# A trunk kernel on one core: six turns per mixer moved from TensorE to transposing DMAs on ScalarE's queue

## The chip, the core and the metric

The kernel runs on one core of a Trainium2 chip. Times are microseconds (us) of device time of that core. Five engines run their own instruction streams, in order: TensorE (PE; its weight loads are listed as PEld), VectorE (DVE), ScalarE (ACT), GpSimd (POOL) and SyncE (SP, which here only issues DMAs). They wait for each other by semaphores. Lower is better.

## The reference

Two layers over x of 256 tokens by 1024 features, in float32. Each layer is a half-step feed-forward network (FFN), a mixer, and a second half-step FFN, each with a norm before and after it. The mixer projects the normed x to 3080 columns and splits them:

```
da_q, da_k, da_v, ml_qk, ml_v, ml_o, ml_g = jnp.split(proj, SPLIT_IDX, axis=-1)
y_da = _diff_attention(da_q, da_k, da_v, lam_vecs, subln_g, lam_init)
y_ml = _mlstm(ml_qk, ml_v, ml_o, ml_g, conv_w, conv_b, gate_b, ml_norm_g)
y = jnp.concatenate([y_da, y_ml], axis=-1).astype(h.dtype)
return y @ w_out
```

In the attention half, queries and keys are rotated (each 64-wide head by position), the queries are scaled by 1/8, and the scores of two softmaxes per head are combined. In the other half, ml_qk (512 columns) goes through a causal convolution of width 4 along the tokens, then silu, and gives queries and keys of a gated linear recurrence. Attention scores and the convolution need the features on partitions, while the projection gives tokens on partitions: so rotated queries, rotated keys and ml_qk have to be turned (transposed), each for both blocks t of 128 tokens. These are six turns of 128 x 512 in each mixer.

## The kernel before

Every float32 product is made of three matmuls: weights and activations are split into a rounded part (wh, hh) and the rest (wl, hl). Weights come in pieces of 1 MB (wr, three buffers) on SP's queue. For each half of a piece ACT makes wh (line 288) and DVE makes wl (line 289). Lines 401 to 403 are the three matmuls.

**FFN.** Its 11 chunks of 256 hidden columns are walked one after the other. After silu and product, the hidden values h are turned by a DMA: ACT writes the two 16-bit words of each float apart into planes (line 535), SP issues a transposing DMA from planes to a tile turned (line 537), and DVE joins the words again into hT (line 539). The last chunk is computed in turned form and needs no turn, so one FFN has ten.

**Mixer.** The function traverse walks the projection in steps of one k (three matmuls) and puts the other work between them: the tuple AT gives, for each stage in the list of stages, the step ahead of which it is written down. A scheduler then orders each engine's stream. The stages of interest:

- conv_input(t) copies ml_qk of token block t out of PSUM into nat (line 895). conv_input_t(t) turns nat by four PE transposes into a PSUM bank ptr (line 879, in the function transposed), and ACT copies the bank into xpad (line 899). Then conv runs on DVE (line 910).
- rope(pin, t) copies a query or key block to rv (ACT, line 1057), and DVE rotates it: lines 1058, 1063 twice, and the sum at line 1064 into ra. roped(i, t) turns ra by four PE transposes, and ACT copies the bank into qkT with a scale (line 1071).
- The gate stages: gate_copy (line 930, ACT), gate_inputs (PE line 939, DVE lines 940 and 942), gate_logs (ACT), gate_log_f (DVE line 957, into g2), gate_rows (PE line 967, four transposes of g2), gate_chain (DVE from line 973 on).
- weighted_qk (PE lines 1023 to 1031, DVE lines 1028, 1027, 1033), scores (PE line 1094; DVE lines 1097 and 1098), combine (DVE line 1122, PE line 1124).

Names: pieces 35 and 36 are the weights of the queries, 37 and 38 those of the keys. q0, q1, k0, k1 below are the rotated query and key blocks t = 0, 1. The tag "ev" has five buffers for nat, ra, rb, rv, h, planes, turned, hT and others. The tag "bk" has four PSUM banks.

Of the kernel before, what the change touches and what calls it, by code (L numbers as in the profile page):

```python
# [19 lines left out]
U16 = mybir.dt.uint16  # L20
AF = mybir.ActivationFunctionType
ALU = mybir.AluOpType
# [3 lines left out]
P = 128  # L26
D = 1024
S = 256
NT = S // P
# [10 lines left out]
AT = (0, 2, 6, 6, 7, 22, 24, 24, 24, 24, 36, 40, 24, 46, 34, 50, 43, 52, 52, 57, 61, 60, 61, 67, 67, 69, 71, 78, 74, 74, 78, 84)  # L40
# [91 lines left out]
class _Trunk:  # L132
# [397 lines left out]
    def ffn_planes(self, h):  # L530


        nc = self.nc
        planes = self.t2("planes", (P, 2, 512), U16)
        nc.scalar.activation(planes, h.rearrange("p t j -> p (t j)").bitcast(U16).rearrange("p (n u) -> p u n", u=2), AF.Copy)
        turned = self.t2("turned", (P, 8, P), U16)
        nc.sync.dma_start_transpose(turned, planes.rearrange("p u n -> p (u n)"))
        hT = self.t2("hT", (P, 4, P))
        nc.vector.tensor_copy(hT.rearrange("p b n -> p (b n)").bitcast(U16).rearrange("p (n u) -> p u n", u=2),  # L539
                              turned.rearrange("p (u b) n -> p u (b n)", u=2))  # L540
        ops = [self.ffn_operand() for _ in range(NT)]
        for t in range(NT):
            self.ffn_hilo(hT[:, 2 * t:2 * t + 2], *ops[t])
        return [[tuple(v[:, k] for v in ops[t]) for k in range(2)] for t in range(NT)]

# [157 lines left out]
    def mixer(self, pre, gi_post):  # L703
        m = _Mixer(self, pre, gi_post // 3)
# [10 lines left out]
        m.conv_input_t(0)  # L715
# [42 lines left out]
class _Mixer:  # L758


    def __init__(self, tr, pre, l):
        self.tr, self.l = tr, l
        self.xT, self.r = pre
        self.yT = [[None, None] for _ in range(NT)]
        self.conved = None
        self.rot, self.qkT, self.so, self.p = [], [], [], {}
# [62 lines left out]
    def stages(self):  # L829
# [6 lines left out]
            self.gate_rows,  # L836
            self.gate_chain,
# [6 lines left out]
            lambda: self.roped(0, 0, 0.125),  # L844
            self.conv_silu,
            lambda: self.roped(0, 1, 0.125),
            self.weighted_qk,
            lambda: self.roped(1, 0, 1.0),
            lambda: self.scores(0, 0),
            self.intra_weights,  # L850
            lambda: self.roped(1, 1, 1.0),
# [37 lines left out]
    def conv_input(self, t, pin):  # L889
        tr = self.tr  # L890
        if t == 0:
            self.xpad = tr.xpad
        nat = tr.t2("nat")
        with tr.tc.high_priority():
            self.act(nat, pin, AF.Copy, scale=self.r[t])
        self.nat = nat

    def conv_input_t(self, t):
        self.act(self.xpad[:, :, 3 + t * P:3 + (t + 1) * P], self.transposed(self.nat), AF.Copy)
# [152 lines left out]
    def rope(self, pin, t):  # L1052
        tr, tt = self.tr, self.tt
        v, a, b = tr.t2("rv"), tr.t2("ra"), tr.t2("rb")
        v8, a8, b8 = (i.rearrange("p (g d) -> p g d", g=8) for i in (v, a, b))
        with tr.tc.high_priority():
            self.rv = self.act(v, pin, AF.Copy, scale=self.r[t])
# [7 lines left out]
        self.rot.append(a)  # L1065

    def roped(self, i, t, scale):

        if t == 0:
            self.qkT.append(self.tr.t4("qkT", (P, 4, S)))  # L1070
        self.act(self.qkT[i][:, :, t * P:(t + 1) * P], self.transposed(self.rot[2 * i + t]), AF.Copy, scale=scale)
# [185 lines left out]
```

## Time and profile before

| what | value |
|---|---|
| median of 3 runs | 962.49 us (962.29 to 962.94) |
| the profiled execution, its own time | 962.02 us |
| its span, first to last instruction | 960.2 us |
| PE busy | 952.8 us (99%) |
| DVE busy, ACT busy | 638.7 us, 571.2 us |
| granted TensorE clock, mean | 0.999 |
| transposing DMAs | 40, all issued by SP |
| first mixer, second mixer | about 195 to 290 us, about 668 to 763 us |

A row of the timeline gives start, duration, engine, line, operation, and names out<-in; "x4" stands for four in a row, then the duration is from the first start to the last end. In brackets stands how long the engine had been idle and who ended that. A row of the table of groups gives busy time, mean ns of one, and idle time before. Matmuls overlap in the records: one of 512 columns lasts 0.39 us, but the next starts 0.23 us later. A neighbour on DVE or ACT may start about 0.08 us before the one ahead has ended.

### The profile page before, as it was taken

How to read it: one execution, taken by the hardware profiler on the slowest of the kernel's cores; microseconds unless marked ns; L12 is line 12 of the kernel's file. 1: busy time of each engine (PE TensorE's matmuls, PEld its weight loads, DVE VectorE, ACT ScalarE, POOL GpSimd, SP SyncE). 2: the span in 40 equal slices, each digit the busy share in tenths (PEclk: the TensorE clock that was granted, in tenths of full speed). 3: DMA queues.
4: the chain of work that ended last, by engine and by line, in shares of the span. 5: the costliest groups of instructions: out<-in, count | busy, mean ns of one | idle time of the engine just before them, and what ended most of it. 6: DMA issues, size and time to landing. Idle time of an engine off the chain costs nothing.

```text
span 960.2 us, 12037 instructions
## 1 busy us (share of the span) xinstructions
PE 952.8 (99%) x4523; PEld 788.9 (82%) x4523; DVE 638.7 (67%) x945; ACT 571.2 (59%) x937; POOL 29.5 (3%) x55
## 2 busy tenths in 40 slices
PE   9999999999999999999999999999999999999997
PEld 7888888888888888888888888888888888888885
DVE  6765655689867766555687555566988676755553
ACT  8755554577856655454476555555778466555542
POOL 2000000000010000000000000000001000000000
PEclk9999999999999999999999999999999999999999
DMA  8996656236352975676458666653454257765621
GB/s 317 328 288 202 225 193 219 105 132 241 116 192 91 299 245 193 218 247 176 154 189 283 206 225 208 196 187 128 172 202 174 90 182 256 272 205 192 225 72 44
DMA packets 69879, 189.32 MB, mean 197 GB/s; under 512 B 45274, under 2 KB 46426, under 8 KB 49086
## 3 DMA queue, kind: packets, MB, share of 16 engines
q1 hardware_dynamic: 69246, 187.95, 58.0%
q8 instruction: 35, 0.57, 0.2%
q10 hardware_dynamic: 576, 0.61, 0.2%
q14 instruction: 22, 0.18, 0.1%
HBM read 177.01 MB, written 1.05 MB: 185 GB/s over the span
## 4 chain that ended last, share of the span: by engine, by line
PE 97%; DVE 1%; DMA 1%; ACT 0%; issue 0%; POOLq 0%; DVEq 0%; ACTq 0%
PE pin L401 13%; PE pin L402 13%; PE pin L403 13%; PE bk L401 10%; PE bk L402 10%; PE bk L403 10%; PE ptr L402 6%; PE ptr L403 6%; PE ptr L401 6%; PE pin L610 1%; PE ptr L610 1%; PE ptr L879 1%; PE ptr L427 1%; DMA wr<-in_w_dram 1%; PE bk L1094 1%; PE ptr L615 1%
## 5 line engine op out<-in xcount | busy, mean ns | idle before, releaser
L289 DVE TENSOR_TENSOR wl<-wr,wh 128x1024 fp32r<-128x1024 f32 x324 | 389.2, 1221 | 180.4 <-ACT wh L288 174.4
L288 ACT ACTIVATE wh<-wr 128x1024 fp32r<-128x1024 f32 x324 | 333.9, 1055 | 171.2 <-DMA wr<-in_w_dram 44.1
L401 PE MATMUL pin<-wh,both 128*128 128x512 f32 x560 | 221.2, 396 | 0.0
L403 PE MATMUL pin<-wh,both 128*128 128x512 f32 x560 | 218.3, 390 | 0.0
L402 PE MATMUL pin<-wl,both 128*128 128x512 f32 x560 | 218.2, 390 | 0.0
L401 PE MATMUL bk<-wh,hh 128*128 128x512 f32 x352 | 137.4, 390 | 0.1
L402 PE MATMUL bk<-wl,hh 128*128 128x512 f32 x352 | 137.0, 389 | 0.0
L403 PE MATMUL bk<-wh,hl 128*128 128x512 f32 x352 | 136.9, 389 | 0.0
L403 PEld LDWEIGHTS pin<-wh,both 128*128 128x128 f32 x560 | 105.1, 188 | 22.3
L401 PEld LDWEIGHTS pin<-wh,both 128*128 128x128 f32 x560 | 105.3, 188 | 22.0 <-issue 0.7
L402 PEld LDWEIGHTS pin<-wl,both 128*128 128x128 f32 x560 | 105.3, 188 | 20.6
L403 PE MATMUL ptr<-wh,both 128*128 128x512 f32 x256 | 99.4, 389 | 0.0
L402 PE MATMUL ptr<-wl,both 128*128 128x512 f32 x256 | 99.4, 389 | 0.0
L401 PE MATMUL ptr<-wh,both 128*128 128x512 f32 x256 | 98.9, 389 | 0.0
L401 PEld LDWEIGHTS bk<-wh,hh 128*128 128x128 f32 x352 | 66.1, 188 | 14.0 <-ACT hh L550 0.5
L403 PEld LDWEIGHTS bk<-wh,hl 128*128 128x128 f32 x352 | 66.1, 188 | 13.7
L402 PEld LDWEIGHTS bk<-wl,hh 128*128 128x128 f32 x352 | 66.1, 188 | 13.5
L539 DVE COPY hT<-turned 128x1024 uint16<-128x1024 uint16 x40 | 30.3, 757 | 41.9 <-DMA turned<-planes 41.5
L401 PEld LDWEIGHTS ptr<-wh,both 128*128 128x128 f32 x256 | 48.1, 188 | 10.0
L402 PEld LDWEIGHTS ptr<-wl,both 128*128 128x128 f32 x256 | 48.1, 188 | 10.0
L550 ACT ACTIVATE hh<-hT 128x256 fp32r<-128x256 f32 x80 | 28.9, 409 | 46.0 <-DVE hT L539 46.0
L403 PEld LDWEIGHTS ptr<-wh,both 128*128 128x128 f32 x256 | 48.1, 188 | 9.9
(210 smaller groups left out, 891.9 us busy)
## 6 DMA issues: line engine op xcount, KB each, us to landing
wr<-in_w_dram SPq DMA_DIRECT2D x162, 1024.0 KB, 5.2
gpost<-in_gpost_dram SPq DMA_DIRECT2D x6, 512.0 KB, 6.3
wr<-in_w_dram SPq DMA_DIRECT2D x2, 512.0 KB, 6.1
wr<-in_w_dram SPq DMA_DIRECT2D x3, 256.0 KB, 4.3
x<-in_x_dram SPq DMA_DIRECT2D x3, 256.0 KB, 4.4
turned<-planes SPq DMA_TRANSPOSE x40, 4.4
out_dram<-x SPq DMA_DIRECT2D x2, 256.0 KB, 2.1
x<-in_x_dram SPq DMA_DIRECT2D x2, 128.0 KB, 3.0
```

Source lines behind the costliest of these rows:

```text
L288: ia = nc.scalar.activation(hi, raw[:, j], AF.Copy)
L289: iv = nc.vector.tensor_tensor(lo, raw[:, j], hi.bitcast(F32), op=ALU.subtract)
L401: mm(ps, xh, wh, start=start, stop=False)
L402: mm(ps, xh, wl, start=False, stop=False)
L403: mm(ps, xl, wh, start=False, stop=stop)
L427: nc.tensor.transpose(ptr[:, k, :], x[:, (4 * hf + k) * P:(4 * hf + k + 1) * P], self.ident)
L539: nc.vector.tensor_copy(hT.rearrange("p b n -> p (b n)").bitcast(U16).rearrange("p (n u) -> p u n", u=2), turned.rearrange("p (u b) n -> p ...
L550: self.nc.scalar.activation(hh, h, AF.Copy)
L610: self.nc.tensor.matmul(b, self.cols(w[kh], k)[0][:, c], both[kh][:, k].rearrange("p i t -> p (i t)"), start=kh == 0 and k == 0, stop=Fals ...
L615: self.nc.tensor.matmul(b[:, 0:NT * P], self.cols(w[kh], k)[1][:, c], both[kh][:, k, 0:NT].rearrange("p i t -> p (i t)"), start=False, sto ...
L879: self.T(ptr[:, b, :], a[:, b * P:(b + 1) * P], self.tr.ident)
L1094: self.mm(pcs[c][:, h, :], self.qkT[0][rows, h0 + h, t * P:(t + 1) * P], self.qkT[1][rows, h0 + h, 0:nk], start=True, stop=True)
```

## The change

The six turns of each mixer leave PE. A new function turn(v, queue, planes) does what ffn_planes did, but sends the transposing DMA back into the tile v itself, whose words are already in planes; joined(out, turned) is the copy on DVE that puts the words together, in the mixer straight into xpad or qkT. In the mixer the queue is ScalarE's, so ACT issues these DMAs; rb serves as planes for the rotated blocks. The scale 1/8 of the queries moves from the copy into qkT to the copy into rv, with a small extra DVE instruction for its factor (rhalf). FFN keeps SP's queue and now also turns in place, so the tile turned is gone. AT is renumbered for the stages whose place changes.

```diff
-AT = (0, 2, 6, 6, 7, 22, 24, 24, 24, 24, 36, 40, 24, 46, 34, 50, 43, 52, 52, 57, 61, 60, 61, 67, 67, 69, 71, 78, 74, 74, 78, 84)
+AT = (0, 2, 6, 6, 7, 20, 22, 24, 24, 24, 24, 36, 40, 28, 46, 34, 50, 46, 52, 52, 57, 61, 60, 61, 67, 67, 69, 71, 78, 74, 74, 78, 84)
...
+    def turn(self, v, queue, planes=None):
+        planes = (planes if planes is not None else self.t2("planes")).bitcast(U16).rearrange("p (u n) -> p u n", u=2)
+        u16 = v.bitcast(U16)
+        self.nc.scalar.activation(planes, u16.rearrange("p (n u) -> p u n", u=2), AF.Copy)
+        turned = u16.rearrange("p (b n) -> p b n", b=8)
+        queue.dma_start_transpose(turned, planes.rearrange("p u n -> p (u n)"))
+        return turned
+
+    def joined(self, out, turned):
+        self.nc.vector.tensor_copy(out.bitcast(U16).rearrange("p b (n u) -> p u b n", u=2),
+                                   turned.rearrange("p (u b) n -> p u b n", u=2))
...
-        m.conv_input_t(0)
...
             self.gate_rows,
+            lambda: self.conv_input_t(0),
             self.gate_chain,
...
             self.act(nat, pin, AF.Copy, scale=self.r[t])
-        self.nat = nat
+        self.nat.append(tr.turn(nat, tr.nc.scalar))
...
-        self.act(self.xpad[:, :, 3 + t * P:3 + (t + 1) * P], self.transposed(self.nat), AF.Copy)
+        self.tr.joined(self.xpad[:, :, 3 + t * P:3 + (t + 1) * P], self.nat[t])
...
+        scale = self.r[t]
+        if len(self.rot) < NT:
+            scale = tr.small("rhalf", (P, 1))
+            self.ts(scale, self.r[t], 0.125, None, op0=ALU.mult)
...
-        self.rot.append(a)
+        self.rot.append(tr.turn(a, tr.nc.scalar, b))
...
-        self.act(self.qkT[i][:, :, t * P:(t + 1) * P], self.transposed(self.rot[2 * i + t]), AF.Copy, scale=scale)
+        self.tr.joined(self.qkT[i][:, :, t * P:(t + 1) * P], self.rot[2 * i + t])
```

Three places in the streams show what the scheduler made of it (the second mixer has the same rows under other numbers). In brackets stand the semaphores that a row waits for: of an engine by its name, of a DMA as DMAHW.

First, DVE at the start of the first mixer, before: the second half of the pre-norm of token block 1, piece 36, the gate inputs, piece 37, g2, and the first row of the gate chain.

```order
L433 TENSOR_TENSOR both_179_1700<-xg_199_1829,both_179_1700 128x4x128 [waits Activation_49]
L289 TENSOR_TENSOR wl_36_0_1863<-wr_36_1861,wh_36_0_1864 128x1024 [waits DMAHW5_49,Activation_49]
L289 TENSOR_TENSOR wl_36_1_1867<-wr_36_1861,wh_36_1_1868 128x1024 [waits Activation_49]
L940 TENSOR_REDUCE gs_208_1896<-bk_207_1895 128x16 [waits PE_49]
...
L289 TENSOR_TENSOR wl_37_0_1982<-wr_37_1980,wh_37_0_1983 128x1024 [waits DMAHW6_49,Activation_49]
L957 SCALAR_TENSOR_TENSOR g2_591<-gn_209_1897,lg_210_1917 128x4x4 [waits Activation_49]
L957 SCALAR_TENSOR_TENSOR g2_591<-gn_209_1897,lg_210_1917 128x4x4
L289 TENSOR_TENSOR wl_37_1_1992<-wr_37_1980,wh_37_1_1993 128x1024 [waits Activation_49]
L973 SCALAR_TENSOR_TENSOR gt_221_2011<-c_scan_570,bk_211_1931 100x256 [waits PE_49]
```

The same place now:

```order
L433 TENSOR_TENSOR both_169_1690<-xg_190_1822,both_169_1690 128x4x128 [waits Activation_49]
L551 COPY xpad_608<-nat_185_1803 128x2x4x128 [waits DMAHW0_49]
L289 TENSOR_TENSOR wl_36_0_1850<-wr_36_1848,wh_36_0_1851 128x1024 [waits DMAHW5_49,Activation_49]
L289 TENSOR_TENSOR wl_36_1_1854<-wr_36_1848,wh_36_1_1855 128x1024 [waits Activation_49]
L948 TENSOR_REDUCE gs_198_1883<-bk_197_1882 128x16 [waits PE_49]
...
L289 TENSOR_TENSOR wl_37_0_1976<-wr_37_1974,wh_37_0_1977 128x1024 [waits DMAHW6_49,Activation_49]
L289 TENSOR_TENSOR wl_37_1_1986<-wr_37_1974,wh_37_1_1987 128x1024 [waits Activation_49]
L965 SCALAR_TENSOR_TENSOR g2_588<-gn_199_1884,lg_200_1904 128x4x4 [waits Activation_49]
L965 SCALAR_TENSOR_TENSOR g2_588<-gn_199_1884,lg_200_1904 128x4x4
L981 SCALAR_TENSOR_TENSOR gt_214_2010<-c_scan_567,bk_201_1918 100x256 [waits PE_49]
```

The join into xpad stands ahead of piece 36 and waits for its DMA, and both halves of piece 37 now stand ahead of g2.

Second, DVE ahead of the scores, before: the rotation of k0 (ra_234) and k1 (ra_238), and qd, whose reading sets a PSUM bank free.

```order
L289 TENSOR_TENSOR wl_41_1_2250<-wr_41_2223,wh_41_1_2251 128x1024 [waits Activation_49]
L1064 TENSOR_TENSOR ra_234_2100<-ra_234_2100,rb_235_2101 128x512 [waits DVE_49]
L1058 TENSOR_TENSOR ra_238_2136<-rv_237_2135,c_1_568 128x512 [waits Activation_49]
L1063 TENSOR_TENSOR rb_239_2137<-rv_237_2135,c_1_568 128x8x32 x2
L289 TENSOR_TENSOR wl_42_0_2324<-wr_42_2322,wh_42_0_2325 128x1024 [waits DMAHW4_49,PE_49,Activation_49]
L289 TENSOR_TENSOR wl_42_1_2334<-wr_42_2322,wh_42_1_2335 128x1024 [waits Activation_49]
L1064 TENSOR_TENSOR ra_238_2136<-ra_238_2136,rb_239_2137 128x512 [waits DVE_49]
L289 TENSOR_TENSOR wl_43_0_2409<-wr_43_2407,wh_43_0_2410 128x1024 [waits DMAHW5_49,Activation_49]
L1028 SCALAR_TENSOR_TENSOR qd_607<-qk_606,bk_244_2229 128x256 [waits PE_49]
```

And now (ra_205 is q0, ra_210 q1, ra_225 k0, ra_228 k1):

```order
L551 COPY qkT_223_2074<-ra_205_1944 128x2x4x128
L289 TENSOR_TENSOR wl_41_1_2233<-wr_41_2206,wh_41_1_2234 128x1024 [waits Activation_49]
L289 TENSOR_TENSOR wl_42_0_2302<-wr_42_2300,wh_42_0_2303 128x1024 [waits DMAHW6_49,PE_49,Activation_49]
...
L551 COPY qkT_223_2074<-ra_210_1991 128x2x4x128 [waits DMAHW1_49]
L1076 TENSOR_TENSOR ra_225_2089<-ra_225_2089,rb_226_2090 128x512 [waits DVE_49]
...
L1076 TENSOR_TENSOR ra_228_2122<-ra_228_2122,rb_229_2123 128x512 [waits DVE_49]
L289 TENSOR_TENSOR wl_42_1_2312<-wr_42_2300,wh_42_1_2313 128x1024 [waits Activation_49]
L551 COPY qkT_232_2191<-ra_225_2089 128x2x4x128 [waits DMAHW3_49]
L289 TENSOR_TENSOR wl_43_0_2387<-wr_43_2385,wh_43_0_2388 128x1024 [waits DMAHW0_49,Activation_49]
L1036 SCALAR_TENSOR_TENSOR qd_604<-qk_603,bk_233_2212 128x256 [waits PE_49]
```

Two joins (q0, q1) and the first half of piece 42 now stand ahead of the sum of k0, and the join of k0, which waits for its DMA, stands ahead of the first half of piece 43 and of qd. The join of k1 follows three rows later, ahead of the first row of the scores on DVE (line 1109).

Third, ACT at the same place, now:

```order
L260 ACT_TABLE_LOAD
L545 ACTIVATE rb_226_2090<-ra_225_2089 128x1024 [waits DMAHW7_49,DVE_49]
L288 ACTIVATE wh_42_1_2313<-wr_42_2300 128x1024 [waits PE_49]
L547 DMA_TRANSPOSE ra_225_2089<-rb_226_2090 128x8x128 [waits Activation_49]
L545 ACTIVATE rb_229_2123<-ra_228_2122 128x1024 [waits DVE_49]
L288 ACTIVATE wh_43_0_2388<-wr_43_2385 128x1024 [waits DMAHW0_49,PE_49]
L547 DMA_TRANSPOSE ra_228_2122<-rb_229_2123 128x8x128 [waits DMAHW5_49,Activation_49]
```

Where one copy out of PSUM (line 1071) stood for each block, there are now a copy into planes and the issue of a DMA, with one other row between them.

More of the change, by code (lines that the diff above doesn't have):

```diff
@@ L530, in ffn_planes @@
     def ffn_planes(self, h):
[L533 to L537, printed above, removed]
         hT = self.t2("hT", (P, 4, P))
-        nc.vector.tensor_copy(hT.rearrange("p b n -> p (b n)").bitcast(U16).rearrange("p (n u) -> p u n", u=2),
-                              turned.rearrange("p (u b) n -> p u (b n)", u=2))
+        self.joined(hT, self.turn(h.rearrange("p t j -> p (t j)"), self.nc.sync))
         ops = [self.ffn_operand() for _ in range(NT)]
@@ L765, in __init__ @@
         self.conved = None
-        self.rot, self.qkT, self.so, self.p = [], [], [], {}
+        self.nat, self.rot, self.qkT, self.so, self.p = [], [], [], [], {}
         self.aT, self.lsum, self.hn, self.y = [None] * NT, [None] * NT, [None] * NT, [None] * NT
@@ L843, in stages @@
             lambda: self.conv((0, 1)),
-            lambda: self.roped(0, 0, 0.125),
+            lambda: self.roped(0, 0),
             self.conv_silu,
-            lambda: self.roped(0, 1, 0.125),
+            lambda: self.roped(0, 1),
             self.weighted_qk,
-            lambda: self.roped(1, 0, 1.0),
+            lambda: self.roped(1, 0),
             lambda: self.scores(0, 0),
             self.intra_weights,
-            lambda: self.roped(1, 1, 1.0),
+            lambda: self.roped(1, 1),
             lambda: self.scores(1, 0),
@@ L1055, in rope @@
         v8, a8, b8 = (i.rearrange("p (g d) -> p g d", g=8) for i in (v, a, b))
+        scale = self.r[t]
+        if len(self.rot) < NT:
+            scale = tr.small("rhalf", (P, 1))
+            self.ts(scale, self.r[t], 0.125, None, op0=ALU.mult)
         with tr.tc.high_priority():
-            self.rv = self.act(v, pin, AF.Copy, scale=self.r[t])
+            self.rv = self.act(v, pin, AF.Copy, scale=scale)
             i = tt(a8, v8, tr.rope[:, 0, t, :].unsqueeze(1).broadcast_to([P, 8, 64]), op=ALU.mult)
@@ L1064, in rope, with roped @@
             self.turned = tt(a, a, b, op=ALU.add)
-        self.rot.append(a)
-    def roped(self, i, t, scale):
+        self.rot.append(tr.turn(a, tr.nc.scalar, b))
+    def roped(self, i, t):
         if t == 0:
             self.qkT.append(self.tr.t4("qkT", (P, 4, S)))
-        self.act(self.qkT[i][:, :, t * P:(t + 1) * P], self.transposed(self.rot[2 * i + t]), AF.Copy, scale=scale)
+        self.tr.joined(self.qkT[i][:, :, t * P:(t + 1) * P], self.rot[2 * i + t])
     def values_da(self, pin, t):
```

## The prediction, made before the result was known

> **What bounds the kernel now.** I read the page first, then the table by stretches, then the rows of each engine around the six turns of the first mixer.
>
> ```profile
> span 960.2 us, 12037 instructions
> PE 952.8 (99%) x4523; PEld 788.9 (82%) x4523; DVE 638.7 (67%) x945; ACT 571.2 (59%) x937; POOL 29.5 (3%) x55
> PE 97%; DVE 1%; DMA 1%; ACT 0%; issue 0%; POOLq 0%; DVEq 0%; ACTq 0%
> ```
>
> PE is busy for 99% of the span and makes up 97% of the chain that ended last. So time that leaves PE leaves the kernel, and a wait on PE is paid in full. But in the stretch of the mixer where the turned blocks are made, DVE is as full as PE (columns: stretch, length and PE, PEld, DVE, ACT, POOL, clock, DMA):
>
> ```profile
> 210.00:220.00 10.00, 10.00 (x50) 8.31 (x49) 9.75 (x17) 7.31 (x12) 0.00 (x0) 1.00 0.30 116
> 220.00:230.00 10.00, 10.00 (x48) 8.25 (x47) 10.00 (x20) 9.39 (x14) 0.00 (x0) 1.00 0.51 189
> 230.00:240.00 10.00, 10.00 (x51) 8.06 (x49) 9.05 (x15) 6.58 (x7) 0.00 (x0) 1.00 0.75 278
> ```
>
> That decides the case: the change takes from PE and gives to DVE and ACT, in a stretch where DVE has nothing left.
>
> **What leaves PE.** Four transposes of one block, between matmuls of 512 columns (timeline, PE):
>
> ```profile
> 225.85 0.40 PE L403 MATMUL pin<-wh,both 128*128 128x512 f32 x1
> 226.09 0.60 PE L879 MATMUL ptr<-c,ra 128*128 128x128 f32 x4
> 226.44 0.49 PE L401 MATMUL pin<-wh,both 128*128 128x512 f32 x1
> 226.76 0.39 PE L402 MATMUL pin<-wl,both 128*128 128x512 f32 x1
> ```
>
> From 226.09 to 226.76 is 0.67; an undisturbed matmul takes its 0.23 of that (225.85 to 226.09 is such a step), so a turn costs PE 0.44. Six turns in each of two mixers: 12 x 0.44 = 5.3 us. That is all there is to gain.
>
> **What comes in its place.** Per turn: a copy into planes on ACT, the issue of a DMA on ACT's own stream, the flight, and a join on DVE; the eviction from PSUM goes. All have rows in the FFN or the mixer:
>
> ```profile
> L535 ACT ACTIVATE planes<-h 128x1024 uint16<-128x1024 uint16 x40 | 42.1, 1052 | 8.6 <-DVE h L528 8.4
> L539 DVE COPY hT<-turned 128x1024 uint16<-128x1024 uint16 x40 | 30.3, 757 | 41.9 <-DMA turned<-planes 41.5
> L1071 ACT ACTIVATE qkT<-ptr 128x512 f32<-128x512 f32 x8 | 4.8, 603 | 0.1
> L537 SPq DMA_TRANSPOSE turned<-planes x40: 1237/1238/3697, 23.6 to 923.0; - x40
> DMA to landing us min/median/max: 2.7/4.4/8.9
> ```
>
> The issue holds SP's stream for 1.24; no row shows it on ACT. Its cost there lies between 0 (hidden behind the row dispatched ahead of it) and 1.24; I take 1.24 from the end of planes, the same instruction's row, but let the one ACT row between planes and issue run beside it. ACT's new work is then at most 1.05 + 1.24 - 0.60 = 1.69 per turn, 10.1 per mixer. The flight is 2.7 at best from issue to landing, 4.4 in the middle; I take 2.7 wherever no weight load is in flight by its turn, and keep 4.4 as the other end. Each join takes 0.76, some 0.68 net, since neighbours on DVE overlap by about 0.08.
>
> A page of the Trainium skill speaks against the whole change: "VectorE: DVE Perf Modes" advises in its rules for kernel authors to transpose 128x128 on TensorE where PSUM will do as target, and lists 1309 ns for a DMA turn of such a block of bf16 in its section on the three transpose paths. Eight such blocks one after the other would be an estimate of 10.5 us; the trace disagrees on the size, 2.7 for the eight blocks of one DMA, but by that figure the first two waits priced below would each be 7.8 longer in both mixers, some 31 us more; as the trace has the size itself, I give that no chance.
>
> **The weights** can slip. The two rows below are the second half of piece 40, counted down both engines' orders: DVE makes it, PE uses it.
>
> ```profile
> 226.45 1.22 DVE L289 TENSOR_TENSOR wl<-wr,wh 128x1024 fp32r<-128x1024 f32 x1
> 235.46 0.39 PE L402 MATMUL pin<-wl,both 128*128 128x512 f32 x1
> ```
>
> Made by 227.67, used at 235.46: 7.8 ahead. The DVE slip below is under 5, so this cover holds and I cost it at nothing; if the slip passed 7.8, each further us would be a us of PE. What has no such lead are the gates and the scores.
>
> **First wait: the gate rows.** ACT, DVE and PE at the start of the mixer:
>
> ```profile
> 194.82 0.69 ACT L895 ACTIVATE nat<-pin,rs 128x512 f32<-128x512 f32 x1 [1.11 <-POOL rs L416]
> 196.64 1.23 ACT L432 ACTIVATE both<-xg 128x512 fp32r<-128x512 f32 x2 [1.13 <-DVE xg L431]
> 198.85 2.36 DVE L289 TENSOR_TENSOR wl<-wr,wh 128x1024 fp32r<-128x1024 f32 x2 [0.25 <-ACT wh L288]
> 202.14 0.19 DVE L940 TENSOR_REDUCE gs<-bk 128x16 f32<-128x32 f32 x1 [0.93 <-PE bk L939]
> 203.36 1.22 DVE L289 TENSOR_TENSOR wl<-wr,wh 128x1024 fp32r<-128x1024 f32 x1 [0.24 <-ACT wh L288]
> 204.50 0.25 DVE L957 SCALAR_TENSOR_TENSOR g<-gn,lg 128x16 f32<-128x16 f32 x2
> 205.39 0.60 PE L967 MATMUL bk<-c,g 128*100 128x128 f32 x4
> ```
>
> Before, g2 is done at 204.75, 0.64 ahead of PE. Now: nat ends at 195.51, planes at 196.6; the DMA is issued beside the first of the two rows L432 and lands at 196.65 + 2.7 = 199.4 (a weight load sharing the engines would make that later). DVE waits for it with the join, which stands ahead of piece 36: join 199.4 to 200.1, piece 36 until 202.45, gs at 202.4 and, as long as before (202.14 to 203.12, without its 0.24 of idle), piece 37 from 203.4. Both halves of it stand ahead of g2 now, 2.36, so g2 is done at 205.95. PE, 0.44 earlier by the missing turn, is there at 204.95: it waits **1.0**. Behind it are the gate transposes, all matmuls that follow, and on DVE the gate chain.
>
> **Second wait: the scores.** PE needs q0 and k0 in qkT; the second score matmul needs the bank that qd reads. Rows around it:
>
> ```profile
> 231.53 0.68 DVE L1064 TENSOR_TENSOR ra<-ra,rb 128x512 f32<-128x512 f32 x1
> 233.40 2.35 DVE L289 TENSOR_TENSOR wl<-wr,wh 128x1024 fp32r<-128x1024 f32 x2
> 238.34 0.42 DVE L1028 SCALAR_TENSOR_TENSOR qd<-qk,bk 128x256 f32<-128x256 f32 x1 [0.84 <-PE bk L1023]
> 239.98 1.16 PE L1094 MATMUL bk<-qkT,qkT 64*128 64x128 f32 x16
> ```
>
> The sum of k0 ends at 232.21 before. Now the gate chain starts 0.55 later (PE's 1.0 less 0.44), DVE has no idle time until here to make it up, and ahead of the sum stand three joins (xpad of block 1, q0, q1: 2.04), half of piece 42 (2.35 - 1.22 = 1.13) and two rhalf (about 0.2): 232.21 + 0.55 + 3.4 = 236.15. Then planes to 237.2, issue and flight 2.7 to 239.9, join to 240.7. PE arrives at 239.98 - 5 x 0.44 + 1.0 = 238.8, so it waits 1.9 for the first score. The second waits for qd, behind the join and half of piece 43: 240.6 + 1.13 + 0.42 = 242.2. Together **3.4**.
>
> **Third wait: the weighted softmax.** From the first row of the scores on DVE to the product that PE turns:
>
> ```profile
> 239.28 1.22 DVE L289 TENSOR_TENSOR wl<-wr,wh 128x1024 fp32r<-128x1024 f32 x1
> 241.25 0.27 DVE L1097 MEMSET bk<- 64x256 f32 x1 [0.76 <-PE bk L1094]
> 247.32 1.14 DVE L1122 SCALAR_TENSOR_TENSOR p<-p,c 128x128 f32<-128x128 f32 x4
> 248.06 0.78 PE L1124 MATMUL ptr<-c,p 128*128 128x128 f32 x4
> ```
>
> Before, the first of the four products is done near 247.7, PE comes at 248.06: no slack worth the name. Now qd starts at 241.8, the half of piece 43 at 242.7 (as before 0.94 after qd), then the join of k1 from 243.85, and the MEMSET, which PE has released by 243.4 (242.2 + 1.16), only at 244.5. From there 6.07 as before, less 0.22 of idle that falls away, and 0.41 for the first product: 250.8. PE gets from its second score to this place in 248.06 - 239.98 - 0.44 = 7.64, at 249.8: it waits **1.0** more. After that both engines are shifted alike and I see no further wait; PE has no idle time in which to win any of this back.
>
> **The sum.** Per mixer -6 x 0.44 + 1.0 + 3.4 + 1.0 = +2.8; the second mixer has the same rows 473.68 later, so I count it twice: 962.02 (the profiled execution: its span of 960.2 and 1.8 around it) + 5.6 = 967.6. The median shown, 962.49, lies 0.5 above that execution, so a median of about 968. FFN's turn in place I cost at nothing either way: the same copy, DMA and join with one buffer less, and behind them the matmuls of the chunks that stand between a turn and its use; without that cover each of the 40 turns could cost or give back a join, 0.76.
>
> **Rivals.** *It gains, all hidden* (not slower): the one question is whether k0's join ends before PE comes for the scores. If issue and join cost DVE and ACT almost nothing, so that the join ended by 237.8 (239.98 - 2.2), and g2 by 204.95, PE would keep its 5.3: 957. For it: PE is the bound, and the weights lead by 7.8. Against: it needs k0 three us earlier than the rows give, and 2.7 of flight plus 0.76 are in the way by themselves. *It cancels*: only the first score waits (1.9), the gate wait shrinks to 0.7 and the third to nothing, since qd's bank or the order matters less than I read: 2.6 against 2.64, 962. For it: each is a reading of one row of waits; against: the waits stand in the streams. *Contended*: k0's and k1's flight share the engines with weight loads, 4.4 for 2.7, and the issue starts only when the row ahead has ended: 1.7 to 2.7 more per mixer, 971 to 973. For it: DMA is busy for 0.75 of 230 to 240; against: weight loads are freed by DVE rows that have slipped as well. *The weights' lead is used up*, as ACT has up to 10.1 more to do and its idle time is small where it is 9.39 full: that decides from 7.8 of slip on; 3 us past it would make 2 x 3 = 6 more, 974.
>
> **Chances.** Forecast (964.5 to 971) 0.62; cancels (960.5 to 964.5) 0.13; contended or worse (over 971) 0.15; gains 0.10. The range that leaves out the gain and the upper end beyond contention is 962 to 973; the likeliest case alone, 964.5 to 971. A measurement here tells 0.2%, about 1.9 us, from no change: faster 0.14 (gains, and a part of cancels), same 0.07, slower 0.79.
>
> **What would show it.** In the changed profile: PE waiting for DVE's g2 (now line 965) about 1.0 and for the scores (line 1106) about 3.4 in each mixer, and for the products of line 1134 about 1.0; the copies of line 551 into qkT idle for a DMA; DVE without idle time from 207 to 236. Issue rows on ACT's queue of 1.24, flights of 2.7. I am wrong if PE waits less than 2.6 per mixer: then k0's join came early, or DVE made up time, and the turn's missing 0.44 stays a gain.

## The result and the profile after

The changed kernel takes 976.34 us (median of 4 runs, 974.54 to 977.55) against 962.72 for the kernel before on the same chip (4 runs, 962.29 to 963.23): a ratio of 1.014, 95% interval 1.0122 to 1.0158. It is 13.6 us slower. The forecast said slower, by 5.5; 976.34 lies above the range of 962 to 973. The profiled execution took 975.72. One execution of e6 below, at a granted clock of 0.556, took 1604.42 and is left out of e6's numbers.

The head of the page, and PE's busy time and clock by slices, of the kernel after:

```profile
span 973.9 us, 12022 instructions
PE 954.8 (98%) x4475; PEld 787.5 (81%) x4475; DVE 647.2 (66%) x961; ACT 577.1 (59%) x937; POOL 31.1 (3%) x55
PE   9999999997999999999999999999979999999997
PEclk9999999998999999999999999999989999999999
```

PE ran 48 matmuls fewer (4475 for 4523; a turn is four) and was still busy 2.0 us longer, in a span 13.7 longer. In the slices, PE and its clock both dip in the same two places, one in each mixer. Who is waited for there, PE's table of waits says (in total, times, longest one):

```profile
PE pin L401 <- ACT rv L1069: 10.0, 2, 5.1
PE bk L975 <- DVE g L965: 1.3, 2, 0.7
```

The first row is a wait that the prediction does not have; the second is its first wait, the gate rows; its second wait, the scores (line 1106, DVE), is missing. PE at the new place in the first mixer, in the changed kernel:

```profile
230.22 0.39 PE L403 MATMUL pin<-wh,both 128*128 128x512 f32 x1
235.55 0.79 PE L401 MATMUL pin<-wh,both 128*128 128x512 f32 x1 [4.94 <-ACT rv L1069]
236.14 0.63 PE L402 MATMUL pin<-wl,both 128*128 128x512 f32 x1
236.57 0.63 PE L403 MATMUL pin<-wh,both 128*128 128x512 f32 x1
...
240.68 0.40 PE L401 MATMUL pin<-wh,both 128*128 128x512 f32 x1
```

PE stands for 4.94 us because it needs the PSUM bank that holds k1's projection, and ACT has not yet copied that bank out to rv. Then the matmuls follow each other by 0.43 (236.14 to 236.57) instead of 0.23. ACT, same kernel and place:

```profile
227.53 1.04 ACT L545 ACTIVATE rb<-ra 128x1024 uint16<-128x1024 uint16 x1
228.48 1.04 ACT L288 ACTIVATE wh<-wr 128x1024 fp32r<-128x1024 f32 x1
228.60 1.25 ACTq L547 DMA_TRANSPOSE ra<-rb  x1
231.13 1.06 ACT L266 ACTIVATE qk<-conv 128x1024 f32<-128x1024 f32 x1 [1.61 <-DVE conv L918]
234.81 0.69 ACT L1069 ACTIVATE rv<-pin,rs 128x512 f32<-128x512 f32 x1 [2.62 <-DMA ra<-rb]
```

This is the cause, and it has two parts. The first: ACT is free at 232.19 and its next instruction, the copy of k1 into rv, starts at 234.81, released by a transposing DMA: that of q1, issued at 228.60. It reads rb, q1's planes. rv, ra, rb and planes all come from the tag "ev" with five buffers, and the rv of k1 is due in a buffer that q1's turn still holds. That is 2.62 of the 4.94. The second part is the other 2.3: had the buffer been free, the copy would still have started at 232.19 and not at 230.6, when PE was done with the bank, since in ACT's order it stands behind the silu (row L266), and the silu waits for the convolution on DVE, whose last row ends at 231.09. The two rows in the kernel before, where the convolution ended at 228.07 and the copy waited for nobody's DMA:

```profile
228.10 1.06 ACT L266 ACTIVATE qk<-conv 128x1024 f32<-128x1024 f32 x1 [0.27 <-DVE conv L910]
229.07 0.67 ACT L1057 ACTIVATE rv<-pin,rs 128x512 f32<-128x512 f32 x1
```

In the order of ACT, with the semaphores in brackets, the new wait for the buffer can be read without a run (before, then now):

```
L1057 ACTIVATE rv_237_2135<-pin_232_2064,rs1_204_1840 128x512 [waits PE_49]
L1069 ACTIVATE rv_227_2121<-pin_222_2051,rs1_195_1833 128x512 [waits DMAHW1_49]
```

The flight of q1 took 6.2, from issue to the release of rv. Weight loads and the turns of q0 to k1, issues with their median time to landing (changed kernel, 205 to 250):

```profile
wr<-in_w_dram SPq DMA_DIRECT2D x7, 1024.0 KB, 5.0
ra<-rb ACTq DMA_TRANSPOSE x4, 6.2
```

A weight load was issued at 228.40, 0.20 ahead of q1's DMA, and landed at 233.76: the two shared the DMA engines. The granted clock, same kernel, in stretches of 3.41 us (columns: stretch, length and PE busy, clock, DMA share, GB/s):

```profile
230.24:233.65 3.41, 0.36 (x2) 1.00 0.87 311
233.65:237.07 3.42, 1.52 (x4) 0.50 0.92 263
237.07:240.48 3.41, 3.41 (x10) 0.50 0.46 140
240.48:243.89 3.41, 3.41 (x17) 1.00 0.65 141
```

The clock is granted in full for the first 3.0 us of the idle time, then halved, and stays halved until about 240.5, 5 us after PE has work again. The Trainium skill, "TensorE: Matmul & The Clock Gate", Part 1, "What's actually happening", describes this gate (half rate after an idle window of about 3.4 us, full rate again after as long a busy one); this place agrees on the halving and on the step (0.43), and the half clock lasts two such lengths, 6.83.

**Where 6.8 us per mixer come from.** I compared the start of the n-th projection matmul in both traces, first mixer, and read off where the difference changes:

| place | us |
|---|---|
| at entry, from the FFN ahead | +0.27 |
| L935 waits for the pre-norm, less nat0's turn | 0.42 - 0.44 |
| gate rows (first wait) | +0.87 |
| turns of nat1, q0, q1 gone | -1.36 |
| wait for the bank of k1 | +5.10 |
| twelve matmuls at half clock | +2.40 |
| k0's turn gone | -0.44 |
| k1's turn gone, third wait | -0.48 + 0.49 |
| at exit | +6.83 |

The second mixer enters at 6.83 and leaves at 13.95 with the same rows (gate 0.85, bank 5.23, half clock 2.87). The two mixers give the whole difference in span, 13.7.

### The profile page after: what moved, and what is told of

Same layout as the page of the kernel before. It is cut to its first block, busy times and chain, and to the rows that moved or that the text cites. A ratio compares the mean times of both kernels' runs of the same rounds, so it can differ in the third digit from the quotient of the medians.

```text
span 973.9 us, 12022 instructions
## 1 busy us (share of the span) xinstructions
PE 954.8 (98%) x4475; PEld 787.5 (81%) x4475; DVE 647.2 (66%) x961; ACT 577.1 (59%) x937; POOL 31.1 (3%) x55
## 4 chain that ended last, share of the span: by engine, by line
PE 95%; DMA 2%; ACT 1%; DVE 1%; issue 0%; SPq 0%; ACTq 0%; POOLq 0%; DVEq 0%
PE pin L401 13%; PE pin L402 12%; PE pin L403 12%; PE bk L401 10%; PE bk L402 10%; PE bk L403 10%; PE ptr L401 6%; PE ptr L402 6%; PE ptr L403 6%; PE pin L618 2%; PE ptr L618 2%; DMA ra<-rb 1%; PE ptr L427 1%; PE pin L623 1%; PE ptr L623 1%; DVE wl L289 1%
## 5 line engine op out<-in xcount | busy, mean ns | idle before, releaser
L401 PEld LDWEIGHTS pin<-wh,both 128*128 128x128 f32 x560 | 106.5, 190 | 33.5 <-ACT rv L1069 10.9
L403 PEld LDWEIGHTS pin<-wh,both 128*128 128x128 f32 x560 | 106.4, 190 | 22.9
L403 PEld LDWEIGHTS bk<-wh,hl 128*128 128x128 f32 x352 | 66.1, 188 | 13.7
L551 DVE COPY hT<-h 128x1024 uint16<-128x1024 uint16 x40 | 30.3, 757 | 47.9 <-DMA h<-planes 47.7
```

Source lines behind the costliest of these rows:

```text
L401: mm(ps, xh, wh, start=start, stop=False)
L403: mm(ps, xl, wh, start=False, stop=stop)
L551: self.nc.vector.tensor_copy(out.bitcast(U16).rearrange("p b (n u) -> p u b n", u=2), turned.rearrange("p (u b) n -> p u b n", u=2))
```

## The experiments

Two theories stood first. *Buffers*: the wait is the one on the buffer that q1's DMA holds; without it the forecast's own three waits come out and the time is near 968. *Data*: the turned data themselves come too late, and any order of buffers leaves the time near 976. Each kernel was timed against the kernel before on the same chip, in that chip's own runs. "Order-only" means that an instruction was held behind another of the same engine, to keep the streams otherwise near to what they were. The edits are shown cut, and where a stage moves, AT is renumbered too. Of the thirteen times expected, e1 and e8 came in the range of the theory that was put first and e4 0.3 below it; the other ten missed it.

### e1: only k1's rv in another buffer

The copy of k1 goes into the buffer aT0, which is free at that time; order-only constraints keep the rows of pieces 42 and 43 and the copies of the values in their places.

```diff
-        v, a, b = tr.t2("rv"), tr.t2("ra"), tr.t2("rb")
+        v, a, b = tr.t2("aT0" if len(self.rot) == 3 else "rv"), tr.t2("ra"), tr.t2("rb")
```

> The changed kernel with one buffer wait taken away: the tile rv of the last rotated key block, k1, lies in the buffer of aT0 (free until the combination of the scores), not in the pool that the planes of q1 lie in; a few order-only dependencies keep ACT's and DVE's rows from there on close to the order of the changed kernel. THEORY BUFFER (the copy of k1 out of PSUM waited for q1's transposing DMA only because it takes over the buffer that this DMA reads; that held a PSUM bank for which PE idled 5 us, and the matmuls after it ran at half clock): PE's wait for rv at line 401 of the changed kernel is gone, no matmul of 0.63 us is left there, and what remains is the gate wait of 1.1 to 1.5 and a wait for k0's join ahead of the scores of 1.5 to 3 per mixer; 964 to 968 us. RIVAL LOAD (ACT and DVE have too much to do in this stretch, and the bank is only where it shows): the same 5 us turn up in the next wait, the scores or the next bank, with the half clock behind them; 973 to 977 us.

Measured: 966.22 (965.22 to 967.23) against 961.89, ratio 1.0045 (1.003 to 1.006). Of the 13.6 us, 4.3 are left. PE's waits in this kernel:

```profile
PE bk L1115 <- DVE qkT L557: 3.5, 2, 1.9
PE bk L981 <- DVE g L971: 3.3, 2, 2.5
PE ptr L1145 <- DVE p L1143: 1.1, 2, 0.8
```

The wait for the bank is gone, and in its place stand the three waits of the prediction, in its order. In the first mixer, single rows:

```profile
205.74 0.64 PE L981 MATMUL bk<-c,g 128*100 128x128 f32 x4 [0.72 <-DVE g L971]
240.48 1.16 PE L1115 MATMUL bk<-qkT,qkT 64*128 64x128 f32 x16 [1.87 <-DVE qkT L557]
249.01 1.11 PE L1145 MATMUL ptr<-c,p 128*128 128x128 f32 x4 [0.81 <-DVE p L1143]
```

0.72, 1.87 and 0.81, where the prediction had 1.0, 1.9 (then 1.5 more for qd) and 1.0. What it had not: in the second mixer the gate waits 2.54, since nat0's DMA flew 4.8 (issue at 671.68, DVE released at 676.47) and not 2.7:

```profile
671.68 1.25 ACTq L553 DMA_TRANSPOSE nat<-planes  x1
676.47 0.77 DVE L557 COPY xpad<-nat 128x1024 uint16<-128x1024 uint16 x1 [2.14 <-DMA nat<-planes]
```

Behind that wait the matmuls run 0.43 apart for 3.7 us, 1.6 more than undisturbed. The sum: 7.9 of waits, 1.6 of half clock, 5.3 of turns gone, +4.2. The traced execution's span is 5.1 longer than before, so 0.9 is not in this sum; the median of the four runs is 4.3 longer. Data alone falls. But e1 does not show that the buffer was the whole wait: freed of it, the copy of k1 also moved in ACT's order, to 227.75, ahead of the silu at 230.39, so both parts of the wait went at once. e5 and e12 keep it behind the silu.

### e2 and e3: one half of the change each

e2 turns only nat by DMA, e3 only queries and keys; the other blocks go through TensorE as before.

```diff
 e2, rope / roped
-        self.rot.append(tr.turn(a, tr.nc.scalar, b))
+        self.rot.append(a)
...
-        self.tr.joined(self.qkT[i][:, :, t * P:(t + 1) * P], self.rot[2 * i + t])
+        self.act(self.qkT[i][:, :, t * P:(t + 1) * P], self.transposed(self.rot[2 * i + t]), AF.Copy, scale=scale)
```
```diff
 e3, conv_input / conv_input_t
-        self.nat.append(tr.turn(nat, tr.nc.scalar))
+        self.nat = nat
...
-        self.tr.joined(self.xpad[:, :, 3 + t * P:3 + (t + 1) * P], self.nat[t])
+        self.act(self.xpad[:, :, 3 + t * P:3 + (t + 1) * P], self.transposed(self.nat), AF.Copy)
```

> Only the convolution's input is turned by a DMA on ACT's queue; the rotated queries and keys are turned by PE as before. FFN's turn in place. THEORY BUFFER: no transposing DMA is left that rv of k1 could wait for, so the long PE wait is absent; two turns less are worth 2 x 2 x 0.44 = 1.8 us, the gate wait of 1.1 to 1.5 per mixer stays; 963 to 965 us. RIVAL LOAD (the loss spreads over all turns with the issue and the join of each): a third of the 13.6 us, 966 to 968 us.

> Only the rotated queries and keys are turned by DMAs on ACT's queue; the convolution's input is turned by PE as before. FFN's turn in place. THEORY BUFFER: rv of k1 still takes over the buffer of q1's planes, so the bank wait with its half clock stays whole, some 7 us per mixer, while the gate wait is gone; eight turns less give back 3.5 us; 972 to 975 us. RIVAL LOAD: two thirds of the 13.6 us and less work on ACT and DVE ahead of the place; 968 to 972 us, with a bank wait well under 4 us.

e2: 968.07 (967.56 to 968.63), ratio 1.0064 (1.0049 to 1.0079). e3: 977.45 (975.83 to 979.19), ratio 1.0156 (1.0139 to 1.0173). PE's waits, first of e2, then of e3:

```profile
PE bk L975 <- DVE g L965: 3.3, 2, 2.6
PE ptr L887 <- DVE ra L1072: 3.0, 4, 1.3
```
```profile
PE bk L1106 <- DVE qkT L551: 12.1, 2, 6.1
PE pin L401 <- ACT rv L1069: 4.3, 4, 1.9
```

Neither half is a gain, and they do not add up to the whole (+6.2 and +15.6, together +13.6). e2 has no bank wait, as the buffer theory wants, but its time is nearest to the rival's 968; it loses at the gate (0.68, then 2.58 where nat0 flew 4.9) and where the PE turns that it kept wait for a DVE that runs late. e3's time is that of the changed kernel, but its wait is elsewhere: q0's DMA flew 8.7, the join of q0 stood in DVE's stream, and everything behind it came late, k0 with it:

```profile
226.26 0.75 DVE L551 COPY qkT<-ra 128x1024 uint16<-128x1024 uint16 x1 [4.35 <-DMA ra<-rb]
```

So e3 also shows a way of losing as much by the data, through a join that blocks DVE. Both times lie above what the buffer theory gave, and the two theories are not exclusive.

### e4: only FFN's turns in place

The kernel before, with turn and joined of the change for the FFN alone.

```diff
-        turned = self.t2("turned", (P, 8, P), U16)
-        nc.sync.dma_start_transpose(turned, planes.rearrange("p u n -> p (u n)"))
...
+        self.joined(hT, self.turn(h.rearrange("p t j -> p (t j)"), self.nc.sync))
```

> The kernel before, with FFN's turned words in place alone (tile turned gone, the DMA lands in h); the mixer is untouched. BOTH THEORIES: FFN's part is hidden, no change, 962 to 963.5 us. RIVAL FFN (the buffer h is now held until the join, so the next h or the next turn is late): slower by 40 times a tenth of a us or more, 966 us and up, with new waits on PE in the FFN.

961.73 (10 runs, 961.22 to 962.95), ratio 0.9998 (0.9989 to 1.0008). The prediction's zero for this part was right.

### e5: q1's DMA alone in the air

The load of piece 43, which shared the air with q1's DMA, waits until that has landed; order-only constraints as in e1, and qd behind k1's sum.

```diff
         self.load = nc.sync.dma_start(raw.rearrange("p a b -> p (a b)"), self.a["w"][i])
+        if i % PIECES_LAYER == 43:
+            self.tc.add_manual_dep(self.load.ins, self.turned_by["dma", 1].ins.name, ...)
```

> The changed kernel with its buffers as they are, but the weight load of piece 43, which was issued 0.2 us ahead of q1's transposing DMA in the changed kernel, is made to wait until that DMA has landed; order-only dependencies keep the rows of ACT, DVE and PE of the first mixer in the order of the changed kernel. THEORY BUFFER, with the load's share (q1's flight took 6.2 us instead of 2.7 because a weight load shared the DMA engines, and rv of k1 waits for this flight): q1's flight falls to 2.7 to 2.8, rv starts 3.4 us earlier, PE's idle time at the bank falls from 4.9 to about 1.5, no matmul takes 0.63 us after it; 976.3 less 2 x 3.4 less 2 x 2.2 is 965, and as the scores' wait takes a part of it back, 965 to 970 us; the load of piece 43 comes 3 to 4 us later and lies within the weights' lead. RIVAL (the flight is long whatever else flies, by its 2-byte packets): flight still above 5, time 975 us or more.

972.54 (971.9 to 973.27) against 962.57, ratio 1.0106 (1.0093 to 1.0119). q1's flight fell from 6.2 to 2.7 in both mixers. PE's waits in e5:

```profile
PE pin L410 <- ACT rv L1078: 5.2, 2, 2.6
PE bk L984 <- DVE g L974: 3.7, 2, 3.0
PE ptr L1148 <- DVE p L1146: 2.7, 2, 2.3
```

The bank wait is halved, 5.1 to 2.6. The half that is left is not a wait for q1's DMA, which landed at 231.41. ACT in e5, first mixer:

```profile
231.27 1.06 ACT L270 ACTIVATE qk<-conv 128x1024 f32<-128x1024 f32 x1 [1.67 <-DVE conv L927]
232.52 0.69 ACT L1078 ACTIVATE rv<-pin,rs 128x512 f32<-128x512 f32 x1 [0.20 <-DVE qkT L560]
```

The copy of k1 follows the silu, which had waited for the convolution on DVE, and then 0.20 for the join of q0; so here it has taken over a buffer of q0, not of q1, and e5 changed more than the flight. What it shows is the second part of the wait by itself: 2.58 and 2.57 in the two mixers. By the rows of the changed kernel a flight of 2.7 would have ended at 231.3, before ACT was free at 232.19; so it takes the long flight and the shared buffer together to make the first part. The time, 972.54, lies between theory and rival: half clock still followed in the first mixer, nat0's second flight was 5.2 and the gate waited 3.0.

### e6 and e10: the joins later in DVE's stream

e6 is e1 with the join of xpad's first block behind g2; e10 is e6 with the joins of q0 and q1 behind the sum of k1.

```diff
 e6
-        self.tr.joined(self.xpad[:, :, 3 + t * P:3 + (t + 1) * P], self.nat[t])
+        self.tr.after(self.tr.joined(self.xpad[:, :, 3 + t * P:3 + (t + 1) * P], self.nat[t]), [self.logs_by])
```
```diff
 e10, beside it
+        if i == 0:
+            self.tr.after(join, [self.turned])
```

> The kernel of e1_k1rv, and the join of the convolution's input of block 0 stands behind the gates' logs (g2) on DVE instead of ahead of piece 36. THEORY (the first wait is as the forecast names it: the join waits at DVE's head for its DMA, and g2 stands behind it): PE's waits for g2 of 0.7 and 2.5 us go, the join falls into the time in which PE turns the gates; the scores' waits stay; 962.5 to 964.5 us. RIVAL (DVE is full from the gates to the scores, so what PE does not wait for at g2 it waits for at the scores): the scores' wait grows by as much; 965.5 to 967 us.

> The kernel of e6_gate with the joins of q0 and q1 behind the sum of k1 on DVE instead of ahead of the sum of k0. THEORY (the scores' wait is DVE's slip to k0's sum plus planes, issue, flight and join, as the forecast's second wait has it): k0's sum comes 1.4 us earlier, its join too, and the scores' wait of 1.9 per mixer falls to about 0.5; 962 to 963.5 us. RIVAL (PE waits for the latest of the flights, and k1's or q1's join is then the last): the wait stays, 964.5 us or more.

e6: 964.99 (5 runs, 964.72 to 965.68), ratio 1.0028 (1.0016 to 1.0039), just above the theory's range and the best of all kernels that turn in the mixer by DMA. e10: 975.1 (974.35 to 975.55), ratio 1.0133 (1.0119 to 1.0147). Waits of e6, then DVE rows of e10 in the first mixer:

```profile
PE bk L1115 <- DVE qkT L557: 3.9, 2, 2.0
PE bk L981 <- DVE g L971: 1.2, 2, 0.7
```
```profile
234.44 0.76 DVE L1081 TENSOR_TENSOR rb<-rv,c 128x256 f32<-128x256 f32 x2 [0.92 <-DMA ra<-rb]
239.91 0.76 DVE L1081 TENSOR_TENSOR rb<-aT,c 128x256 f32<-128x256 f32 x2 [1.66 <-DMA ra<-rb]
```

In e6 the gate wait falls from 3.3 to 1.2: 2.54 to 0.57 in the second mixer, where the join had waited long for nat0 ahead of piece 36, but only 0.72 to 0.67 in the first. There the join was not what decided; both halves of piece 37 still stand ahead of g2, and end no earlier. The scores still cost 3.9: k0's chain of planes, issue, flight and join. In e10, turned data that are read later keep their buffers longer, and now DVE itself waits for a turn's DMA before it may write rb: the buffer wait has moved from ACT to DVE. The joins of q0, q1 and k0 stand behind the sum of k1, end at 243.29, and the scores wait 8.8 in two mixers.

### e7 and e11: only the queries by DMA

Both keep the keys and the convolution's input on TensorE (as in e2 and e3) and take rv of k1 from aT0; the queries, made first, have most time. e7 joins them after the convolution, e11 after the sum of k1, and issues q1's DMA only after the key copies.

```diff
 e11
-        self.rot.append(tr.turn(a, tr.nc.scalar, b))
+        self.rot.append(tr.turn(a, tr.nc.scalar, b) if n == 0 else a)
+        if n == 1:
+            self.q1 = a, b
+        if n == 3:
+            self.rot[1] = tr.turn(self.q1[0], tr.nc.scalar, self.q1[1])
+            tr.after(tr.planes_by, [self.rv])
```

> Only the two query blocks are turned by DMAs; their joins stand behind the convolution on DVE; the keys and the convolution's input are turned by PE as before; rv of k1 lies in the buffer of aT0. FFN's turn in place. THEORY (a turn by DMA pays where its result is wanted 10 us or more later and no buffer or bank waits for its flight): PE loses 4 turns of 0.44, 1.8 us, and waits nowhere: a ratio of 0.998 to the kernel before, 960 to 960.5 us beside 961.9. RIVAL (two more joins and two small rows on a full DVE, 1.6 us per mixer, reach the scores): some of it back or more, 961.5 to 965 us.

> The kernel of e7_q, in which the join of q1 stood idle 2.3 us for its flight at DVE's head and held up k0's sum: here both query joins stand behind k1's sum on DVE, and q1's planes and issue stand behind both copies out of PSUM of the keys on ACT. THEORY (what cost e7_q its gain were rows that waited for a flight at the head of an engine's order): PE waits for neither k0's sum nor rv, four turns less are 1.8 us: 960.3 to 961.3 us beside 962.3. RIVAL (the rows themselves are too many for DVE before the scores): 962.5 us or more.

e7: 968.68 (6 runs, 967.17 to 976.4), ratio 1.0083 (1.0056 to 1.0111). e11: 966.58 (965.47 to 966.77), ratio 1.0041 (1.0027 to 1.0055). DVE in the first mixer of e7:

```profile
235.31 0.76 DVE L1075 TENSOR_TENSOR rb<-rv,c 128x256 f32<-128x256 f32 x2 [2.31 <-DMA ra<-rb]
```

Here q1's DMA flew 7.5 beside a weight load, and k0's rb was due in a buffer that it held: 2.31 of idle DVE. e11 has the same row with 1.23. Even with four of twelve turns, and those with the longest lead, the waits that come with them cost more than the 1.8 us (4 x 0.44) that leave PE.

### e8: the mixer's turns issued by SP

```diff
-        self.nat.append(tr.turn(nat, tr.nc.scalar))
+        self.nat.append(tr.turn(nat, tr.nc.sync))
...
-        self.rot.append(tr.turn(a, tr.nc.scalar, b))
+        self.rot.append(tr.turn(a, tr.nc.sync, b))
```

> The changed kernel with the mixers' six transposing DMAs issued on SP's queue, among the weight loads, instead of ScalarE's. THEORY BUFFER: the queue is not the cause; rv of k1 still waits for q1's DMA. SP issues in order, so no weight load overtakes a turn that waits for its planes: loads come later and the flights share less, but a turn also waits behind loads that wait for a free buffer; the bank wait stays within 3 us of what it was, 970 to 980 us. RIVAL ACT (the issue rows of 1.25 us on ACT's queue, six per mixer, are the loss): with the issue on SP the loss is gone, 962 to 966 us.

977.8 (975.01 to 978.22), ratio 1.0152 (1.0137 to 1.0167): no different from the change. Its waits:

```profile
PE bk L1106 <- DVE qkT L551: 8.3, 2, 4.7
PE pin L401 <- ACT rv L1069: 3.7, 2, 2.2
```

Taking the issue off ACT gains nothing. But the waits are others than in the changed kernel: on SP's queue the two query turns fly 9.1 and 4.7, beside loads again, and PE now waits mostly for a join ahead of the scores. So the total says that SP's queue is no better, not what the issue rows on ACT cost by themselves.

### e9: PE kept awake

Twenty matmuls into a bank that nothing reads are put ahead of the values in each mixer (extra work, 20 x 0.23 = 4.5 us per mixer).

```diff
+            if s == 36:
+                bank = tr.bank_tr()
+                w = tr.cols(ws1[1], 0)[0]
+                for _ in range(FILLED):
+                    fill.append(self.mm(bank, tr.identr, w, start=True, stop=True))
```

> The changed kernel, and 20 matmuls of 512 columns (into a spare PSUM bank of ptr, read by nobody) stand on PE between the last matmul of the keys and the first of the values, where PE idled 5 us for rv of k1; DVE's and ACT's rows move a little with it. The wait itself is not shortened. THEORY CLOCK (the matmuls behind the idle 5 us ran at half the granted clock because PE had been idle, 10 to 12 steps of 0.43 us instead of 0.23 and some smaller ones, 2.2 to 2.5 us per mixer): with PE busy over the wait no step of 0.43 us follows it; 976.3 less 4 to 5 is 971 to 973 us. RIVAL (the half clock comes with the DMA traffic or at any pause of the accumulation): steps of 0.43 us stay, 975 us or more.

975.49 (974.04 to 978.85), ratio 1.0143 (1.0126 to 1.016). It does not settle the price of the clock by time: ACT's and DVE's streams changed, q1's DMA flew 3.5 and rv of k1 ran already at 230.63, so the wait to be filled had itself gone, and new waits came (PE for g 3.6, for the products 3.3). In the traced execution no matmul around the fill ran at half rate, and the mean clock was 0.998 against 0.991. The half clock's price rests on the rows of the changed kernel alone.

### e12 and e13: six buffers

"ev" with six buffers, the room taken from scratch tiles; e12 is the change so, e13 is e11 so, with rv back in "ev".

```diff
-        TAGS[_n] = ("ev", 5)
+        TAGS[_n] = ("ev", 6)
```

> The changed kernel with six buffers instead of five in the pool ev (nat, ra, rb, rv, h, planes, hT and others); the room comes from a scratch tile for squares (one buffer instead of two, ACT only) and two spare tiles. rv of k1 then waits for the sine products of k0 on DVE instead of for q1's DMA. THEORY BUFFER: the bank wait of 5 us falls to the time that DVE needs to those products, 1 to 2 us, and most of the half clock goes; the gate wait stays; the scores' wait comes in as in e1_k1rv; 965 to 970 us. RIVAL (what costs is the number of transfers and joins, not the buffer): 974 us or more.

> The kernel of e11_qlate with six buffers in ev, rv of k1 in ev again. In e11_qlate DVE still stood idle 1.2 us, with k0's sine products waiting for q1's DMA (their buffer rb was the one it reads), and PE waited 1.1 us for k0's sum and 0.4 to 0.6 us for each row behind it. THEORY BUFFER: without that wait k0's sum is 1.2 us earlier, PE waits for nothing of the queries, and the four turns' 1.8 us show: 960 to 962 us beside 962.3. RIVAL (two joins and two rhalf more on DVE delay qd and the scores by themselves): 963 us or more.

e12: 974.7 (970.46 to 977.16), ratio 1.0129 (1.01 to 1.0158). e13: 967.97 (966.08 to 968.7), ratio 1.0053 (1.004 to 1.0065). Two of PE's waits in e12, then ACT's row of k1 in e13:

```profile
PE pin L401 <- ACT rv L1069: 5.7, 2, 2.9
PE ptr L1136 <- DVE p L1134: 3.7, 2, 3.1
```
```profile
231.96 0.69 ACT L1071 ACTIVATE rv<-pin,rs 128x512 f32<-128x512 f32 x1 [2.36 <-DVE rb L1077]
```

Both missed what the buffer theory gave: the wait of PE on rv is halved, not gone, and other waits grow. ACT in e12, first mixer:

```profile
232.76 1.06 ACT L266 ACTIVATE qk<-conv 128x1024 f32<-128x1024 f32 x1 [2.25 <-DVE conv L918]
233.72 0.67 ACT L1069 ACTIVATE rv<-pin,rs 128x512 f32<-128x512 f32 x1
```

With six buffers the copy waits for no DMA: it follows the silu without a gap, and in the second mixer it starts at 714.15, while q1's DMA is in flight until 716.2. The 2.85 that PE waits in each mixer come from the silu's wait for DVE alone. So e12 took away the first part of the wait and left the second, as e5 did. In e13 rv of k1 waits for DVE's reading of another rv.

## Why the prediction was right and wrong

- **Direction: right**, and for the reason given: PE is the bound and 0.44 per turn is all there is to win. The accounting shows it (-1.36 for three turns).
- **What failed is the step "What has no such lead are the gates and the scores".** The copy of k1 out of its PSUM bank has no such lead either: PE needs the bank at once, and waits 4.94 and 5.07 for it (5.1 and 5.2 in the accounting). Two things were left out. One is the buffers: the change adds planes and uses the turned tile itself as the target of its DMA, so q1's planes and block are held until the DMA lands, and the pool of five hands one of them to k1's rv: 2.62 and 2.71. That wait stands in ACT's order of the changed kernel, in words (a wait on a DMA where a wait on PE was). The other is ACT's order: the copy stands behind the silu, which waits for the convolution on DVE, and this was 3.0 late: 2.3 per mixer, left by themselves in e5 and e12 (2.6 and 2.85). The forecast had DVE's slip, but followed it on DVE to the sum of k0 and not through the convolution into ACT.
- **The idle PE's clock was not priced either:** 2.4 and 2.9 per mixer. The forecast costed each wait at its own length. With the bank wait these make 7.5 to 8.1 per mixer, in place of the 3.4 that the second wait was to cost.
- **The flight of 2.7 was mis-sized where it mattered.** The rule used, 2.7 wherever no load is in flight by the turn, is borne out (k0 in the changed kernel: issued 238.52, landed 241.28), but q0, q1 and k1 do fly beside loads there: 6.9, 6.2 and 6.2. The other end, 4.4, was too low as well. The rival *Contended* had this mechanism, but at k0 and k1 and at 1.7 to 2.7 per mixer; here it was q1's flight that counted, 2.62 and 2.71, through the buffer.
- **First wait: right.** 0.66 idle, 0.87 in the accounting, for 1.0. The rows ran in the order told, 0.6 to 0.9 later: join from 200.31 (forecast 199.4; nat0 flew 3.3), g2 done at 206.51 (205.95), PE there at 205.82 (204.95). Of its two parts only piece 37 decided in the first mixer: without the join ahead the wait stays 0.67 (e6). In e1, e2 and e5 it is 2.5 to 3.0 in the second mixer where nat0 flew 4.8 to 5.2, and there it is the join.
- **DVE's slip: right in size,** though not in whom it would reach. k0's sum ends at 236.48 in the changed kernel, at 235.77 in e1, for 236.15.
- **Second wait: absent in the changed kernel, since PE was already 5 to 7 us late by then.** In e1 its first part is 1.87 and 1.64 for 1.9. Its second part, 1.5 for qd, was not tested: in the changed kernel's order qd stands behind k0's join, as the forecast has it, but in e1 it runs at 236.97, ahead of that join.
- **Third wait: 0.81 and 0.31 in e1 for 1.0,** 0.49 in the changed kernel's accounting.
- **FFN at nothing: right** (e4). **The weights' lead: held**, no row of PE waits for piece 40.

Taken together, the forecast of 968 comes near e1 (966.2), the change with the copy of k1 set free. In part that is luck: e1's second wait lacks the 1.5 for qd, and its second gate wait is 1.5 longer than forecast.

What stays open: no kernel measured the half clock's price by time alone. Executions of one kernel give a hint and no price: the changed kernel took 974.54 at a mean clock of 0.996 and 975.72 to 977.55 at 0.990 and 0.991, but e6 took 964.93 at 0.994 and 964.72 and 964.99 at 0.999. Why flights beside loads range from 3.1 to 9.7 is not resolved by these traces. No version with turns by DMA beat the kernel before; e4, which has none in the mixer, is the same as before.

## What to carry to other kernels

When a copy through PSUM becomes a DMA, ask what the DMA still reads and writes until it lands, and who is next in line for that buffer; the new waits on DMA semaphores in the order of each engine list them before any run. When an engine slips, follow the slip into every other engine whose rows wait for it, and to what stands behind those rows: here from DVE's convolution through ACT's silu to a bank that PE needed. Price a transposing DMA beside bulk loads by its slow flights, not by its best. And a stall of a full PE can cost more than its length, as the matmuls behind it may run at half clock.

## What the runs showed that was not expected

- A transposing DMA of 128 x 1024 words of 16 bits takes 2.7 to 2.9 us at its quickest, in e5 for q1 with no weight load issued until it had landed, and up to 9.7 beside weight loads (e8), from ACT's queue as from SP's; its issue holds ACT's queue for 1.25 in most rows, 1.3 to 1.9 in some.
- PE at half clock does not need 3 us of idle time. Rows with 0.63 follow 4.94 and 5.07 of idle in the changed kernel, 2.58 in e5, 2.54 in e1, and in e6 1.92 ahead of the scores; but not 2.85 in e12, and not the 2.57 of e5's second mixer. What decides is where the idle time falls. In these traces the clock changes only at the bounds of stretches of 3.41 us, on a grid that has another place in each execution. e5, first mixer, then second:

```profile
229.91:233.32 3.41, 0.83 (x5) 1.00 0.62 129
233.32:236.74 3.42, 3.42 (x8) 0.50 0.96 400
711.19:714.60 3.41, 1.93 (x9) 1.00 0.35 78
714.60:718.02 3.42, 2.33 (x10) 1.00 0.88 314
```

The 2.58 of idle lie in one stretch and leave PE 0.83 busy there: half clock follows. The 2.57 are split over two, which leaves 1.93 and 2.33: none follows. In all fifteen traces, a stretch at full clock with 1.45 or less of PE's busy time was followed by half clock, one with 1.51 or more was not, and at 1.50 it went either way (half in e6, not in e12). Half clock ended behind a stretch with 3.3 or more of busy time and went on behind one with 2.5 or less, which is why the changed kernel's lasts 6.83 and that of e1 and e6 3.41. So a given stall halves the clock in one execution and not in another. (PE's busy time is modelled in the records, so these bounds are those of the records.)

The Trainium skill, "TensorE: Matmul & The Clock Gate", Part 1, "What's actually happening", calls this window free-running and gives it about 3.4 us; the rows agree. Its section "Why this matters for your kernels" advises no idle gaps over some 3 us; here 1.92 was enough (e6).
